# Scores by 64-row products, a later last join of gate and up, and large tiles for every third page step

## Chip, cores, metric

The kernel runs on one core of a Trainium2 chip. The metric is device time of one execution in microseconds: the median of three runs of the kernel before is 2318.37 us (2318.06 to 2319.26).

## What is computed

One inference step of a two-layer decoder, for a prompt of 1024 tokens and for eight samples of one token each (1032 token columns in all, width 1024, everything in float32 precision). Layer 0 mixes by an S5 state-space model beside differential attention, layer 1 by a gated linear recurrence beside causal pooling; each layer ends in a SwiGLU feed-forward network. What the change touches:

```
proj = rmsnorm(x) @ w_in ; u, q, k, v = split(proj) ; q, k = rope(q), rope(k)   # 8 heads of 64
p = softmax(q k^T / 8, causal), per head       # 4 pairs of heads, components c = 0 and 1
o[h] = (p[2h] - lam * p[2h+1]) @ v[h]          # h = 0..3, values 128 wide
# samples: 2048 past keys and values each, in 16 pages of 128 rows, found through page_table
# feed-forward, in both layers:
x = x + (silu(n @ wg) * (n @ wu)) @ wd         # 2816 hidden columns, n = rmsnorm(x)
```

## The kernel before

TensorE works in products of two halves: an operand is split into a rounded part H and a remainder L, and a product is H·H + L·H + H·L (`mm3`, lines 718 to 720). The program is written as one stream of Python calls; a scheduler turns it into a fixed order for each engine, and each engine then runs its list in that order, waiting on semaphores. What decides the time are therefore the order on each engine and the tiles: a tile belongs to a pool with a number of buffers, and whoever fills a tile waits until the last user of the buffer is done.

**The attention stage** (about 325 to 630 us) is the loop at the end of `mixer0`. `order` runs over G = 0, 1 (queries 0 to 511, 512 to 1023) and the four heads h; each (h, G) has four blocks qi of 128 queries. For a block, `attn_scores` makes the two score matrices (c = 0, 1) of 128 queries by nk = (4G+qi+1)·128 keys, takes the maximum on VectorE (DVE) and the exponential on ScalarE (ACT) into tiles P; `attn_values` combines and transposes them (pT to wT, lines 1338 and 1340) and, after the fourth block, multiplies by the values (po, line 1348). Between these calls the loop places three kinds of other work:

- `vsteps`: 32 *page steps* for the samples (`pv`, line 1453). Step c of group g loads four pages of 256 KB from `in_cv`, one for each of four samples, and runs four products of 32 columns, one after the other on four column groups.
- `fill`: the S5 output path (`s5_mix`: tiles z, f, xr, products pd).
- `late`: the first half of the attention's output projection (`attn_mix`: tiles az, ax).

**Page buffers.** The pool `kv` has `KV_BUFS` = 8 buffers of 128x512, so two page steps. Pages are issued on SyncE's queue (SP), in order, by `load_page`.

**Scores before.** Q and K rows of a component are 64 deep. `attn_load` fills a tile Q whose upper 64 rows hold q's H part and whose lower 64 hold its L part, and tiles K (G = 0) or KH, KL (G = 1) in which both halves hold the same 64 rows of k. One product with all 128 rows then gives H·H + L·H, a second one with KL gives the rest; k is fetched twice for this, in pieces of 64 rows. These loads go out on GpSimd's queue (POOL), two `next(nxt)` for each block (`LOADS`), among the loads and stores of `fill` and `late`. The tiles come from the pool `S` (24 buffers of 128x1032), as do P, wT, xr, z and others.

**Feed-forward.** `gate_up` runs 11 pairs j of gate and up products in seven block products each, then `finish(j, ...)`: `normed(u)` (line 404, two multiplications of 128x1032 by the norm), and g·u (line 409, two more). `down` then reads the hidden tiles back (h), builds operands from them (`operands`, lines 475 to 491) and weights (`down_weights`, lines 514, 515), and accumulates products into x (`acc`, line 583).

Of the kernel before, what the change touches and what calls it, by code (L numbers as in the profile page):

```python
# [8 lines left out]
F32 = mybir.dt.float32  # L9
F32R = mybir.dt.float32r  # L10
# [47 lines left out]
NB = 16 // NI  # L58
QUEUES = ("gpsimd", "sync", "sync", "gpsimd", "gpsimd")
Y_BUFS = 11  # L60
LOADS = (2, 2, 2, 2)
MID = 4
KV_BUFS = 8
DENSE = (1, 1, 1, 1, 1, 1, 1, 1)
# [132 lines left out]
class Ffn:  # L197
# [180 lines left out]
    def gate_up(self, S, pp):  # L378
# [69 lines left out]
        for j in range(1, 11):  # L448
            cg, cu = slots(j), slots(j)
            for v, c in ((0, cg), (1, cu)):  # L450
                w = self.load(v, j, S if v else t.wst)
                got = nxt[2 * j - 2 + v] if 2 * j - 2 + v < AHEAD else None
                for p in ORDER:
                    if p != 2 or got is None:
                        self.product(p, w, c, pp, got=got if p == 1 else None)
                if self.l + v == 0 and j == 5:
                    with t.after(self.lastf):
                        t.lru_consts()
                if v == 0:
                    normed(cg)  # L460
                    for x in cg[:2]:
                        nc.scalar.activation(x, x, AF.Silu)
            finish(j, cg, cu)

    def operands(self, h, grp, S):

# [51 lines left out]
    def down(self, xs, S, pp, chunks):  # L518
# [72 lines left out]
        def load_x(n):  # L591
            for m in range(len(xs), n):
                xs.append(t.tile(f"x{m}"))
                nc.sync.dma_start(xs[m], self.xd[m])
# [16 lines left out]
        def prep():  # L611
            ci, grp, p, m = weights.pop(0)
            ms = (m, m + 2) if grp and m % 4 == 0 else (m,)
            for j, mm in enumerate(ms):
                if (ci, grp, mm) not in raws:
                    raws[ci, grp, mm] = raw(ci, mm, grp, j), {}
            if ci + grp == 0 and m == 2 and len(xs) < 8:
                load_x(8)
                for j in range(2):
                    nc.sync.dma_start(self.hd[20 + j], self.last[j])  # L620
            made[ci, grp, p, m] = self.down_weights(p, *raws[ci, grp, m])
# [18 lines left out]
class Trunk:  # L640
# [622 lines left out]
    def attn_load(self, h, G):  # L1263

        nc = self.nc
        n = 512 * G + 512
        self.qk = getattr(self, "qk", {})
        Q = self.tile("Q", F32R)[:, :1024].rearrange("p (c n) -> p c n", c=2)
        ks = []
        self.qk[h, G] = (Q, ks)  # L1270
        for half in range(2):
            src = self.qd[h][half][:, G * 512:G * 512 + 512].bitcast(F32R).rearrange("(c p) n -> p c n", c=2)
            nc.gpsimd.dma_start(Q[half * 64:half * 64 + 64], src)
        yield
        for c in range(2):
            if G:
                ks.append([self.tile(t, F32R)[:, :n] for t in ("KH", "KL")])
            else:
                t = self.tile("K", F32R)
                ks.append([t[:, 0:512], t[:, 512:1024]])  # L1280
            for i in range(2):
                for half in range(2):
                    nc.gpsimd.dma_start(ks[c][i][half * 64:half * 64 + 64],
                                        self.kd[h][i][c * 64:c * 64 + 64, :n].bitcast(F32R))
                yield

    def attn_scores(self, h, G, qi):

        nc = self.nc
        Q, ks = self.qk[h, G]  # L1290
        if qi == 0:
            self.sums = getattr(self, "sums", {})
            self.sums[h, G] = self.sm.tile([128, 2, 4], F32, tag="sums", name="sums")
        sm = self.sums[h, G][:, :, qi]
        nk = (4 * G + qi + 1) * 128
        mx = self.sm.tile([128, 2], F32, tag="mx", name="mx")
        both = None if G else self.sc.tile([128, 2, 512], F32, tag="sc", name="sc")
        P2 = None if G else self.tile("P")
        S, P = [], []
        for c in range(2):  # L1300
            KH, KL = ks[c]
            ql = Q[:, c, qi * 128:qi * 128 + 128]
            ps = self.sc.tile([128, 1024], F32, tag="sc", name="sc") if G else both[:, c]
            for k0 in range(0, nk, 512):
                n = min(512, nk - k0)
                last = k0 + n == nk
                o = ps[:, k0:k0 + n]
                nc.tensor.matmul(o, ql, KH[:, k0:k0 + n], start=True, stop=False)  # L1308
                nc.tensor.matmul(o, ql, KL[:, k0:k0 + n], start=False, stop=not last)
                if last:  # L1310
                    nc.tensor.matmul(o[:, n - 128:n], self.identb, self.maskb, start=False, stop=True)
            if G:
                nc.vector.tensor_reduce(mx[:, c:c + 1], ps[:, :nk], AX.X, ALU.max, negate=True)
            S.append(ps[:, :nk])
            P.append(self.tile(f"P{c}")[:, :nk] if G else P2[:, c * 512:c * 512 + nk])
        if not G:
            nc.vector.tensor_reduce(mx, both[:, :, :nk], AX.X, ALU.max, negate=True)
        for c in range(2):
            nc.scalar.activation(P[c], S[c], AF.Exp, bias=mx[:, c:c + 1], accum_out=sm[:, c:c + 1])
# [63 lines left out]
    def sample_steps(self):  # L1383
# [5 lines left out]
        def page(src, b, c):  # L1389
            t = self.kv.tile([128, 512], F32, tag="kv", bufs=KV_BUFS, name="kv")  # L1390
            self.load_page(t, a[src], b * NPAGE + c)
            return t

        def scores(ch):
            def f():
                if ch == 0:
# [49 lines left out]
        def pv(g, c):  # L1446
            def f():
                if c == 0:
                    st["o"] = self.pst("so", self.pq)
                p = st["o"]  # L1450
                vt = [page("cv", 4 * g + j, c) for j in range(4)]
                w = st["s"][c // 8][:, c % 8 * 128:c % 8 * 128 + 128]
                self.row([lambda j=j: nc.tensor.matmul(  # L1453
                    p[32 * j:32 * j + 32, 0:512], w[:, 32 * j:32 * j + 32], vt[j], start=c == 0, stop=False,
# [595 lines left out]
```

## Time and profile before

| | |
|---|---|
| median of three runs | 2318.37 us |
| the profiled execution's own time | 2323.5 us |
| its span, first to last instruction | 2321.7 us |
| mean granted TensorE clock, as a share of full speed | 0.977 |
| TensorE (PE) busy | 2192.2 us, 94% |
| DVE, ACT, POOL busy | 1605.3, 939.3, 477.4 us |
| chain that ended last | PE 79%, DVE 9%, DMA 7% |

The page's slices and the stage table show where PE is not full. The attention stage, 325 to 630 us, has PE busy for 254.24 of 305 us at a mean granted clock of 0.91. The two places between `gate_up` and `down`, near 1120 and 2070 us, have each one stop of PE of 6.6 us. Nearly everything else runs at a full PE.

### The profile page before, as it was taken

How to read it: one execution, taken by the hardware profiler on the slowest of the kernel's cores; microseconds unless marked ns; L12 is line 12 of the kernel's file. 1: busy time of each engine (PE TensorE's matmuls, PEld its weight loads, DVE VectorE, ACT ScalarE, POOL GpSimd, SP SyncE). 2: the span in 40 equal slices, each digit the busy share in tenths (PEclk: the TensorE clock that was granted, in tenths of full speed). 3: DMA queues.
4: the chain of work that ended last, by engine and by line, in shares of the span. 5: the costliest groups of instructions: out<-in, count | busy, mean ns of one | idle time of the engine just before them, and what ended most of it. 6: DMA issues, size and time to landing. Idle time of an engine off the chain costs nothing.

```text
span 2321.7 us, 44913 instructions
## 1 busy us (share of the span) xinstructions
PE 2192.2 (94%) x17529; PEld 2061.1 (89%) x17529; DVE 1605.3 (69%) x3045; ACT 939.3 (40%) x1746; POOL 477.4 (21%) x585
## 2 busy tenths in 40 slices
PE   6999888887989999999899999999999999989998
PEld 6978766655789999999899998899899999989997
DVE  7879435445687557566999878654956565689966
ACT  5233234333664333333444365543633333344331
POOL 5232322222103333332000000000233333300001
PEclk8999998988999999999999999999999999999999
DMA  6488978998543222222765331334232122266512
GB/s 225 144 262 290 258 227 250 280 272 223 183 152 128 91 74 83 68 82 90 292 218 167 104 84 42 102 114 138 76 107 83 67 82 83 74 239 218 192 64 74
DMA packets 145798, 348.21 MB, mean 150 GB/s; under 512 B 33513, under 2 KB 40554, under 8 KB 145586
## 3 DMA queue, kind: packets, MB, share of 16 engines
q1 hardware_dynamic: 112514, 247.18, 32.4%
q0 software_dynamic: 32496, 97.64, 13.6%
q8 instruction: 138, 2.26, 0.4%
q14 instruction: 74, 0.61, 0.1%
q10 hardware_dynamic: 576, 0.52, 0.1%
HBM read 281.17 MB, written 64.08 MB: 149 GB/s over the span
## 4 chain that ended last, share of the span: by engine, by line
PE 79%; DVE 9%; DMA 7%; ACT 2%; issue 2%; SPq 1%; POOL 1%; DVEq 0%; ACTq 0%; POOLq 0%
PE pd L718 23%; PE pd L720 22%; PE pd L719 22%; DMA kv<-in_cv 3%; DMA kv<-in_ck 2%; PE so L1453 1%; PE po L1348 1%; PE pss L1402 1%; DVE wp L312 1%; DMA xr<-in_x 1%; PE pg L1918 1%; PE pT L1338 1%; PE sc L1308 1%; PE pv L1253 1%; PE pv L1254 1%
## 5 line engine op out<-in xcount | busy, mean ns | idle before, releaser
L720 PE MATMUL pd<-b,wp 128*128 128x256 f32 (+1 forms) x3496 | 987.7, 283 | 14.4 <-DVE wp L515 13.2
L718 PE MATMUL pd<-b,wp 128*128 128x256 f32 (+1 forms) x3496 | 991.7, 284 | 7.6 <-DVE c L373 3.5
L719 PE MATMUL pd<-b,wp 128*128 128x256 f32 (+1 forms) x3496 | 990.7, 283 | 2.3 <-DVE b L275 2.3
L720 PEld LDWEIGHTS pd<-b,wp 128*128 128x128 f32 x3496 | 662.3, 190 | 15.4 <-DVE wp L515 13.6
L718 PEld LDWEIGHTS pd<-b,wp 128*128 128x128 f32 x3496 | 662.6, 190 | 11.0 <-ACT wp L311 3.4
L719 PEld LDWEIGHTS pd<-b,wp 128*128 128x128 f32 x3496 | 662.8, 190 | 3.1 <-DVE b L275 3.1
L331 POOL TENSOR_TENSOR as<-wst 128x512 f32<-128x512 f32 x80 | 136.2, 1702 | 487.5 <-DVE wp L312 328.2
L718 PE MATMUL pd<-xh,wh 128*128 128x344 f32 x576 | 191.1, 333 | 14.7 <-ACT wh L691 10.2
L375 ACT COPY c<-pd 128x512 f32<-128x512 f32 (+1 forms) x260 | 106.1, 444 | 223.0 <-PE pd L720 222.7
L720 PE MATMUL pd<-xh,wl 128*128 128x344 f32 x576 | 188.1, 329 | 4.8 <-DVE wl L692 4.7
L719 PE MATMUL pd<-xl,wh 128*128 128x344 f32 x576 | 188.6, 328 | 0.0
L373 DVE TENSOR_TENSOR c<-pd,c 128x512 f32<-128x512 f32 (+1 forms) x214 | 93.3, 470 | 127.0 <-PE pd L720 126.8
L311 ACT CAST wp<-as 128x512 fp32r<-128x512 f32 x176 | 108.8, 621 | 173.0 <-PE pd L720 164.5
L312 DVE TENSOR_TENSOR wp<-wst,wp 128x512 fp32r<-128x512 f32 x122 | 105.4, 867 | 103.7 <-ACT wp L311 103.7
L312 DVE TENSOR_TENSOR wp<-as,wp 128x512 fp32r<-128x512 f32 x176 | 140.3, 800 | 28.0 <-ACT wp L311 27.9
L404 DVE TENSOR_TENSOR c<-c,R 128x1032 f32<-128x1032 f32 x88 | 110.4, 1255 | 44.9 <-ACT c L375 44.9
L718 PEld LDWEIGHTS pd<-xh,wh 128*128 128x128 f32 x576 | 110.0, 191 | 19.3 <-ACT wh L691 10.6
L583 DVE TENSOR_TENSOR x<-pd,x 128x512 f32<-128x512 f32 x160 | 108.3, 688 | 17.1 <-PE pd L720 15.8
L720 PEld LDWEIGHTS pd<-xh,wl 128*128 128x128 f32 x576 | 109.5, 191 | 8.7 <-DVE wl L692 5.9
L719 PEld LDWEIGHTS pd<-xl,wh 128*128 128x128 f32 x576 | 109.9, 191 | 2.1 <-issue 0.2
L691 ACT CAST wh<-wst 128x1024 fp32r<-128x1024 f32 x58 | 60.7, 1046 | 116.7 <-PE pd L719 85.4
L692 DVE TENSOR_TENSOR wl<-wst,wh 128x1024 fp32r<-128x1024 f32 x58 | 70.8, 1221 | 48.3 <-ACT wh L691 47.9
(537 smaller groups left out, 4075.1 us busy)
## 6 DMA issues: line engine op xcount, KB each, us to landing
h<-hd SPq DMA_DIRECT2D x82, 516.0 KB, 5.8
kv<-in_ck SPq DMA_DIRECT2D x128, 256.0 KB, 4.2
kv<-in_cv SPq DMA_DIRECT2D x128, 256.0 KB, 6.1
wst<-in_w_d SPq DMA_DIRECT2D x48, 512.0 KB, 4.2
wst<-in_w_g SPq DMA_DIRECT2D x46, 512.0 KB, 4.1
wst<-in_w_up SPq DMA_DIRECT2D x44, 512.0 KB, 3.5
hd<-c POOLq DMA_DIRECT2D x40, 516.0 KB, 3.0
wst<-in_w_o POOLq DMA_DIRECT2D x28, 512.0 KB, 4.0
```

The costliest lines, as they stand in the source:

```text
L311: nc.scalar.copy(W[:, 0], s)
L312: nc.vector.tensor_tensor(W[:, 1], s, W[:, 0].bitcast(F32), ALU.subtract)
L331: (nc.vector if self.first else nc.gpsimd).tensor_tensor(s, x, y, op)
L373: V.tensor_tensor(o, i, o, ALU.add)
L375: A.copy(o, i)
L404: nc.vector.tensor_tensor(x, x, t.R, ALU.mult)
L583: nc.vector.tensor_tensor(y, pt[:, :, :256], y, add)
L691: nc.scalar.copy(H, src)
L692: nc.vector.tensor_tensor(L, src, H.bitcast(F32), ALU.subtract)
L718: mm(p, WH, XH, start=first, stop=False, **kw)
L719: mm(p, WH, XL, start=False, stop=False, **kw)
L720: mm(p, WL, XH, start=False, stop=last, **kw)
```

## The change

Four edits:

- **Scores.** Q is now a tile with q's H and L parts side by side, each with both components: component c in rows 64c to 64c+63. K, KH and KL hold the two components the same way, each fetched once. A block's scores are three products of 64 rows for each component and chunk of up to 512 keys (H·H, L·H, H·L), c = 0 and c = 1 taking turns, then the two mask products of 128 rows. The list is issued by `row`, which keeps it together after its first product; both score tiles of a block are taken before it. The maxima follow both.
- **Loads.** `attn_load` has four steps of one DMA each (Q's H, K's H, Q's L, K's L), one for each block (`LOADS`), so that K's L part of a head is issued in the block just before the head's first scores.
- **Page steps.** A step with c % 3 == 2 (10 of 32) loads its four pages into two tiles of the pool `S` and not into `kv`.
- **Last join.** `finish(10)` is called in `down`, when the weights of the second m are prepared, and not at the end of `gate_up`.

```
-LOADS = (2, 2, 2, 2)
+LOADS = (1, 1, 1, 1)
...
-            finish(j, cg, cu)
+            if j < 10:
+                finish(j, cg, cu)
+        self.finish = lambda: finish(10, cg, cu)
...
             if ci + grp == 0 and m == 2 and len(xs) < 8:
+                self.finish()
                 load_x(8)
...
-        for half in range(2):
-            src = self.qd[h][half][:, G * 512:G * 512 + 512].bitcast(F32R).rearrange("(c p) n -> p c n", c=2)
-            nc.gpsimd.dma_start(Q[half * 64:half * 64 + 64], src)
-        yield
-        for c in range(2):
...
-            for i in range(2):
-                for half in range(2):
-                    nc.gpsimd.dma_start(ks[c][i][half * 64:half * 64 + 64],
-                                        self.kd[h][i][c * 64:c * 64 + 64, :n].bitcast(F32R))
-                yield
+        for i in range(2):
+            nc.gpsimd.dma_start(Q[:, i], self.qd[h][i][:, G * 512:G * 512 + 512].bitcast(F32R))
+            yield
+            nc.gpsimd.dma_start(ks[i], self.kd[h][i][:, :n].bitcast(F32R))
+            yield
...
+            for j, (q, k) in enumerate(((0, KH), (1, KH), (0, KL))):
+                for c in range(2):
+                    r = slice(64 * c, 64 * c + 64)
+                    calls.append(lambda c=c, r=r, q=q, k=k, j=j, k0=k0, n=n, last=last: nc.tensor.matmul(
+                        S[c][:, k0:k0 + n], Q[r, q, sl], k[r, k0:k0 + n], start=j == 0, stop=j == 2 and not last))
...
+        self.row(calls)
...
+        def wide(g, c):
+
+            T = [self.tile("kv") for _ in range(2)]
+            vt = [T[j // 2][:, j % 2 * 512:j % 2 * 512 + 512] for j in range(4)]
+            for j in range(4):
+                self.load_page(vt[j], a["cv"], (4 * g + j) * NPAGE + c)
+            return vt
...
-                vt = [page("cv", 4 * g + j, c) for j in range(4)]
+                vt = [page("cv", 4 * g + j, c) for j in range(4)] if c % 3 < 2 else wide(g, c)
```

The lines of the changed kernel stand a few numbers higher than those of before (a page step is line 1463 for 1453). On PE, at the start of the attention stage (so: a page step's four products, sc: scores), before:

```order
L1453 MATMUL so<-kv,ss 32x512 x8
L1308 MATMUL sc<-K,Q 128x128
L1309 MATMUL sc<-K,Q 128x128
L1311 LDWEIGHTS identb
L1311 MATMUL sc<-maskb,identb 128x128
L1308 MATMUL sc<-K,Q 128x128
L1309 MATMUL sc<-K,Q 128x128
L1311 LDWEIGHTS identb
L1311 MATMUL sc<-maskb,identb 128x128
```

and now:

```order
L1463 MATMUL so<-kv,ss 32x512 x12
L1310 MATMUL sc<-K,Q 128x128 x6
L1313 LDWEIGHTS identb
L1313 MATMUL sc<-maskb,identb 128x128
L1313 LDWEIGHTS identb
L1313 MATMUL sc<-maskb,identb 128x128
```

Three page steps stand where two stood, and a block's scores are one run of six products with the two masks behind it.

On POOL's queue, the loads for the last head with G = 1 (kd_111 is k of head 3), before:

```order
L1273 DMA Q<-qd_107 64x2x512 x2
L1283 DMA KH<-kd_111 64x1024 x2
L1089 DMA xp_117<-ax 128x512
L696 DMA wst<-in_w_o 128x1024
L1084 DMA ax<-xp_118 128x512
L1283 DMA KL<-kd_111 64x1024 x2
L1283 DMA KH<-kd_111 64x1024 x2
L1356 DMA ao_113<-od 128x512
L1283 DMA KL<-kd_111 64x1024 x2
```

and now:

```order
L1279 DMA Q<-qd_107 128x512 x2
L1092 DMA xp_117<-ax 128x512
L699 DMA wst<-in_w_o 128x1024
L1087 DMA ax<-xp_118 128x512
L1281 DMA KH<-kd_111 128x1024
L1358 DMA ao_113<-od 128x512
L1092 DMA xp_118<-ax 128x512
L1087 DMA ax<-xp_119 128x512
L1281 DMA KL<-kd_111 128x1024
```

Eight loads of 64 rows have become two of 128, and the last of them stands two entries later than before (behind the store of xp_118 and the load of ax from xp_119).

On DVE, between `gate_up` and `down` of layer 0 (b and h: building `down`'s operands, wp: its weights), before:

```order
L404 TENSOR_TENSOR c<-c,R 128x1032
L484 TENSOR_TENSOR h<-h 128x520
L409 TENSOR_TENSOR c<-c 128x1032
L404 TENSOR_TENSOR c<-c,R 128x1032
L476 TENSOR_TENSOR b<-h,b 128x520
L409 TENSOR_TENSOR c<-c 128x1032
L476 TENSOR_TENSOR b<-h,b 128x512
L476 TENSOR_TENSOR b<-h,b 128x520
L482 TENSOR_TENSOR h<-h 128x512
L515 TENSOR_TENSOR wp<-as,wp 128x512
```

and now:

```order
L486 TENSOR_TENSOR h<-h 128x520
L484 TENSOR_TENSOR h<-h 128x512
L517 TENSOR_TENSOR wp<-as,wp 128x512
L478 TENSOR_TENSOR b<-h,b 128x520
L478 TENSOR_TENSOR b<-h,b 128x512
L478 TENSOR_TENSOR b<-h,b 128x520 x2
L486 TENSOR_TENSOR h<-h 128x520
L517 TENSOR_TENSOR wp<-wst,wp 128x512
L517 TENSOR_TENSOR wp<-as,wp 128x512
L478 TENSOR_TENSOR b<-h,b 128x520
L517 TENSOR_TENSOR wp<-as,wp 128x512
L404 TENSOR_TENSOR c<-c,R 128x1032 x2
```

The four joining multiplications stand behind `down`'s first four weights, no longer ahead of them.

## Rows read from the trace of the kernel before

**Rows 1.** The page, part 1: busy time, share and instructions of each engine.
```profile
PE 2192.2 (94%) x17529; PEld 2061.1 (89%) x17529; DVE 1605.3 (69%) x3045; ACT 939.3 (40%) x1746; POOL 477.4 (21%) x585
```
**Rows 2.** Windows: stretch, busy us by engine, PE clock, DMA share, GB/s.
```profile
325.00:630.00 305.00, 254.24 (x1483) 178.63 (x1483) 156.61 (x358) 123.31 (x305) 74.49 (x134) 0.91 0.85 238
345.00:365.00 20.00, 11.02 (x46) 6.13 (x47) 4.94 (x5) 4.21 (x4) 7.92 (x14) 0.66 1.21 299
```
**Rows 3.** Waits, 325 to 630: who waited for whom, total us, times, longest.
```profile
PE so L1453 <- DMA kv<-in_cv: 40.8, 10, 11.6
POOL xp L1089 <- DVE ax L1087: 31.9, 4, 19.2
PE sc L1308 <- ACT P L1319: 4.1, 5, 1.5
SPq L1380 <- PE so L1453: 57.9, 25, 9.2
```
**Rows 4.** Timeline of PE, page steps: start, length, instruction, idle before.
```profile
339.58 1.08 PE L1453 MATMUL so<-kv,ss 128*32 128x512 f32 x4 [5.64 <-DMA kv<-in_cv]
...
362.65 0.64 PE L1453 MATMUL so<-kv,ss 128*32 128x512 f32 x4 [1.67 <-DMA kv<-in_cv]
...
484.10 1.92 PE L1453 MATMUL so<-kv,ss 128*32 128x512 f32 x16
...
496.44 1.08 PE L1453 MATMUL so<-kv,ss 128*32 128x512 f32 x4 [5.95 <-DMA kv<-in_cv]
...
550.56 1.94 PE L1453 MATMUL so<-kv,ss 128*32 128x512 f32 x8 [11.60 <-DMA kv<-in_cv]
```
**Rows 5.** Timeline of SP's queue, 484 to 490.
```profile
485.17 4.76 SPq L1380 DMA_DIRECT2D kv<-in_cv  x8
```
**Rows 6.** Score products by shape (x count), then two in the timeline.
```profile
L1308 PE MATMUL sc<-KH,Q 128*128 128x512 f32 x40 | 18.8, 469 | 3.5 <-ACT P L1319 3.5
...
503.80 0.40 PE L1308 MATMUL sc<-KH,Q 128*128 128x512 f32 x1
504.04 0.40 PE L1309 MATMUL sc<-KL,Q 128*128 128x512 f32 x1
```
**Rows 7.** Timeline of PE: products of 64 rows in the S5 stage.
```profile
58.95 0.38 PE L1679 MATMUL pK<-CL,s5bb 64*16 64x128 f32 x2
59.16 0.39 PE L1677 MATMUL pK<-CL,s5bb 64*16 64x128 f32 x4
59.38 0.39 PE L1679 MATMUL pK<-CL,s5bb 64*16 64x128 f32 x4
...
114.59 0.50 PE L1785 MATMUL py<-U,TG 128*128 128x136 f32 x2
115.02 0.38 PE L1786 MATMUL py<-H,CL 64*128 64x136 f32 x1
115.03 0.38 PE L1788 MATMUL py<-H,CL 64*128 64x136 f32 x1
```
**Rows 8.** DMA issues, 325 to 630: count, KB each, median us to landing.
```profile
wst<-in_w_o POOLq DMA_DIRECT2D x10, 512.0 KB, 6.6
...
KL<-kd POOLq DMA_DIRECT2D x16, 256.0 KB, 9.9
```
**Rows 9.** Timeline of DVE, then of PE, at the end of layer 0's `gate_up`.
```profile
1120.87 1.23 DVE L409 TENSOR_TENSOR c<-c 128x1032 f32<-128x1032 f32 x1
...
1123.82 0.69 DVE L515 TENSOR_TENSOR wp<-as,wp 128x512 fp32r<-128x512 f32 x1
...
1124.57 0.58 PE L720 MATMUL pd<-b,wp 128*128 128x256 f32 x1 [6.59 <-DVE wp L515]
```
**Rows 10.** `down` of layer 0: windows row as in rows 2; PE's waits 1126 to 1345.
```profile
1120.00:1130.00 10.00, 5.43 (x30) 5.43 (x31) 10.00 (x17) 1.53 (x3) 0.00 (x0) 0.66 0.97 341
1180.00:1200.00 20.00, 20.00 (x171) 20.00 (x170) 19.94 (x36) 9.08 (x16) 0.00 (x0) 1.00 0.79 259
...
PE pd L718 <- DVE x L583: 0.9, 2, 0.5
```

More of the change, by code (lines that the diff above doesn't have):

```diff
@@ L1267, in attn_load @@
         self.qk = getattr(self, "qk", {})
-        Q = self.tile("Q", F32R)[:, :1024].rearrange("p (c n) -> p c n", c=2)
-        ks = []
-        self.qk[h, G] = (Q, ks)
-        for half in range(2):
-            src = self.qd[h][half][:, G * 512:G * 512 + 512].bitcast(F32R).rearrange("(c p) n -> p c n", c=2)
-            nc.gpsimd.dma_start(Q[half * 64:half * 64 + 64], src)
-        yield
-        for c in range(2):
[L1276 to L1280, printed above, removed]
-            for i in range(2):
-                for half in range(2):
-                    nc.gpsimd.dma_start(ks[c][i][half * 64:half * 64 + 64],
-                                        self.kd[h][i][c * 64:c * 64 + 64, :n].bitcast(F32R))
-                yield
+        Q = self.tile("Q", F32R)[:, :1024].rearrange("p (i n) -> p i n", i=2)
+        if G:
+            ks = [self.tile(t, F32R)[:, :n] for t in ("KH", "KL")]
+        else:
+            t = self.tile("K", F32R)
+            ks = [t[:, 0:512], t[:, 512:1024]]
+        self.qk[h, G] = (Q, ks)
+        for i in range(2):
[3 more added lines that the diff above has]
+            yield
     def attn_scores(self, h, G, qi):
         nc = self.nc
-        Q, ks = self.qk[h, G]
+        Q, (KH, KL) = self.qk[h, G]
         if qi == 0:
@@ L1296, in attn_scores @@
         mx = self.sm.tile([128, 2], F32, tag="mx", name="mx")
-        both = None if G else self.sc.tile([128, 2, 512], F32, tag="sc", name="sc")
-        P2 = None if G else self.tile("P")
-        S, P = [], []
-        for c in range(2):
[L1301 to L1315, printed above, removed]
@@ L1316, in attn_scores @@
-        if not G:
+        if G:
+            S = [self.sc.tile([128, 1024], F32, tag="sc", name="sc")[:, :nk] for _ in range(2)]
+            P = [self.tile(f"P{c}")[:, :nk] for c in range(2)]
+        else:
+            both, P2 = self.sc.tile([128, 2, 512], F32, tag="sc", name="sc"), self.tile("P")
+            S = [both[:, c, :nk] for c in range(2)]
+            P = [P2[:, c * 512:c * 512 + nk] for c in range(2)]
+        sl = slice(qi * 128, qi * 128 + 128)
+        calls = []
+        for k0 in range(0, nk, 512):
+            n = min(512, nk - k0)
+            last = k0 + n == nk
+            for j, (q, k) in enumerate(((0, KH), (1, KH), (0, KL))):
[3 more added lines that the diff above has]
+                        S[c][:, k0:k0 + n], Q[r, q, sl], k[r, k0:k0 + n], start=j == 0, stop=j == 2 and not last))
@@ L1317, in attn_scores @@
+        for c in range(2):
+            calls.append(lambda c=c: nc.tensor.matmul(S[c][:, nk - 128:nk], self.identb, self.maskb, start=False, stop=True))
+        self.row(calls)
+        if G:
+            for c in range(2):
+                nc.vector.tensor_reduce(mx[:, c:c + 1], S[c], AX.X, ALU.max, negate=True)
+        else:
             nc.vector.tensor_reduce(mx, both[:, :, :nk], AX.X, ALU.max, negate=True)
```

## Prediction

> **What bounds the kernel now.** I began with the busy shares. TensorE is busy for 94% of the span and DVE for 69% [rows 1], so a change pays where TensorE stands still or runs at the low clock, or where it gives TensorE less to do; what it takes from other engines pays only through those. The windows by stage then say where that is. In the attention stage, 325 to 630 us, TensorE is busy for 254.24 of 305 us at a mean granted clock of 0.91 [rows 2]. So 50.8 us are idle, and, with 1.2 GHz at a half, 18% of the stage (0.09 divided by 0.5), 55 us, lies at the low level. The stretch 345 to 365 is the worst of it: 11.02 of 20 us busy at 0.66.
>
> The waits name the cause. Of the idle time 40.8 us, in ten waits, stand before the page steps (line 1453), each for a page of `in_cv` to land [rows 3]. In the timeline they fall into two kinds. Four lie at the start, from 5.64 us at 339.58 to 1.67 us at 362.65 [rows 4], 15.9 us together: there the pages come in no faster than the steps ask. The other six, 25 us, come after steps that stand close together: two steps run back to back at 484.10, only then are their eight buffers free, SP issues the next eight pages from 485.17 on [rows 5], and TensorE comes to the next step before they are in, 5.95 us of idle time at 496.44; the longest, 11.60 us, is at 550.56 [rows 4]. SP's queue shows the other side of it: 57.9 us in which a page load waited for TensorE to leave a buffer [rows 3]. So the limit is the distance between the issue of a page and its use. Throughput is not full: the stage moves 238 GB/s [rows 2], and `down` has 341 GB/s in one stretch [rows 10].
>
> **The page steps** (part 1). Every third step gets eight pages' worth of room outside the pool of eight: its four pages lie in two tiles of `S`. In the new order three steps stand at the start for two, and where two ordinary steps follow each other, the loads of the next are issued with at least two whole steps between, which by the durations of the work on TensorE's list is 14 to 29 us ahead. The new loads wait for tiles of `S`, whose last users lie 14 us of TensorE work or more ahead of the step. Against a landing of about 12 us (485.17 to the end of the wait at 496.44) that covers the 25 us of the later waits. At the start, the third step is loaded ahead and q and k compete with fewer bytes; there I take off a third, 5 of 15.9. That is **-30 us**, with ends of -12 (half of the later waits goes, the start stays) and -40.8.
>
> The clock follows the waits. At the half level a busy microsecond does half a microsecond's work; 55 us at that level, busy for the same share as 345 to 365 (55%), cost some 15 us (half of 55 x 0.55). If the waits in the middle go, about half of it comes back: **-8**, ends 0 and -15.
>
> **The scores** (part 2). Before there are 32 blocks, each with two components of two products for each chunk: 192 products, 96 of them 512 columns wide and the others 256 on average, 73,700 columns. At full clock two products of 512 start 0.24 us apart [rows 6], so all take 34.6 us. Now there are three for two, 288 products of 64 rows and 110,600 columns: 51.8 us one after another (+17), 25.9 us if the upper and the lower half of the rows work at once (-9). The profile shows which: in the S5 stage two products of 64 rows of one kind take 0.21 us (58.95 to 59.16), and four of one half among four of the other take 0.22 (59.16 to 59.38); and at 115.02 and 115.03 products of two kinds start 0.01 us apart [rows 7]. The halves overlap. What the new form adds is the change between products of 128 and of 64 rows: the two at 114.59 hold TensorE until 115.02, 0.43 us [rows 7], where two without a change on either side take 0.21 to 0.23; 0.2 us for each change. A block changes over twice, into its scores and back for the masks: 64 x 0.2 = 13. Together -9 + 13 = **+4**, with ends of -9 (the overlap alone) and +30 (no overlap, and the changes on top).
>
> Here the Trainium skill speaks against this change: its page "TensorEngine Tiling (Array Packing)" (section "Tiling Modes", Key Properties) says that "Changing tiling mode (not just tile) drains the TensorE", where its "Overview" promises work at once for operands of at most 64 rows. By the promise alone the term would be -9. By a full drain, taken as the length of a product beyond its slot (0.40 less 0.24 in the rows above, an estimate), 64 x 0.16 = 10 would make it +1. The row's 0.2 agrees with a drain and a first weight load that nothing hides.
>
> **The loads of q and k.** 80 loads on POOL become 32, and k comes once. This frees POOL and halves the bytes of k, but POOL and DMA bandwidth are not what TensorE waits for today, so I book no gain but that at the start, above. What it adds is a new race. The last load of a head (KL) is now one DMA of 512 KB for G = 1, issued one block ahead of the first scores that use it, and behind stores that wait for DVE: those of line 1089 hold POOL for 31.9 us in four waits [rows 3]. From the work on TensorE's list between the last thing that its issue waits for and its first use, the four heads of G = 1 leave it 7.4, 11.8, 10.7 and 8.4 us. The nearest rows are 6.6 us for a load of 512 KB and 9.9 us for a KL of 256 KB [rows 8]. At 6.6 nothing is exposed; at twice 9.9, 8 to 12.4 us for each head, some 41 in all. The new load has the bytes and the 128 rows of the first of these, but the company of the second; I take 10 to 11 us, which exposes up to 3 us at a head and about 6 in all, and 4 more for issues that come late: **+10**, ends 0 and +41. Behind a score product that waits stands all of TensorE's list, and after it the exponentials and the transposes of the block.
>
> **Both score tiles at once.** A block's scores now want both buffers before the first product, where the first component could start alone. Today TensorE waits 4.1 us in five waits for the exponential that frees one [rows 3]. I take **+3**, ends 0 and +8 (twice today's wait).
>
> **The last join** (part 3). Between `gate_up` and `down` TensorE stops for 6.59 us, until DVE has made the first weight (line 515, 1123.82 to 1124.51) [rows 9], and the clock over 1120 to 1130 is 0.66 [rows 10], 0.34 x 5.43 = 2 us more. Four multiplications of 1.23 us [rows 9], 4.9 us, stand ahead of that weight on DVE's queue; now they stand behind the first four weights. So the stop shrinks by up to 4.9 us, but the work isn't gone: DVE is busy for 10.00 of 10 us there and for 19.94 of 20 in the middle of `down` [rows 10], where today it holds TensorE for only 0.9 us. What is late next are the accumulations of line 583, with 4.9 us more ahead of them, less the time by which TensorE starts sooner. I take 3 us of gain in each layer: **-6**, ends 0 and -14 (stop and clock of one layer, 7, twice).
>
> **SP's queue.** The loads of a wide step wait for tiles of `S` and hold the ordinary pages behind them. By the order these tiles come free in time: **0**, up to +9 (the longest wait of a page load for a buffer today is 9.2 [rows 3]).
>
> **The sum.** -30 - 8 + 4 + 10 + 3 - 6 = -27. The profiled execution's own time is 2323.5 us, so 2296.5; the median of the runs is 0.9978 of it, which gives 2291 us.
>
> **Rivals.**
> *The page waits stay.* If the transfers themselves are what is slow (the DMA engines have a share of 0.85 in the stage and 1.21 in 345 to 365 [rows 2], so they are seldom idle), a third step in flight only makes each page land later. Then only 12 of the 40.8 go, the clock gives back 2, and KL's wait hides among them: -12 - 2 + 4 + 3 - 6 = -13, so 2305 by the median. Against it: the bytes of k halve, and the later waits begin with an issue that came late.
> *The halves don't overlap.* The change would not do what it says: the scores are +30 and not +4, and the sum is -1, 2317. The rows of the S5 stage speak against it, but those products are short.
> *Slower: KL comes late at every head of G = 1.* It needs twice the 9.9 us of the piece of half its size, and POOL issues it behind a store that DVE holds (up to 19.2 us [rows 3]). With 19.8 us against slacks of 7.4 to 11.8 TensorE stops for 8 to 12.4 us at each head, and a stop of this kind brings the low clock, as the one of 6.59 did for 2 us. With 2 us of late issue at each head that is 41 + 8 + 8 = 57. Without the K term the sum is -37, so +20, 2338. It decides from 37 / 4 = 9 us for a head. For it speaks that the last load of k comes close to its use even today; against it, the row of 6.6 us for 512 KB.
> *Better.* KL lands in time, the changes of mode hide behind the products before them, and all the waits in the middle and half of those at the start go: -33 - 10 - 5 + 1 - 8 = -55, 2263.
>
> **How the numbers follow.** The forecast has a chance of 0.60; pages stay 0.13; no overlap 0.07; KL slower 0.08; better 0.12. The range has to leave out no more than 0.2: the slower rival's upper part and the better one's lower end stay outside, so it goes from 2266 (the page, clock and score terms near their good ends) to 2316 (the no-overlap case just out, KL at half of its bad end in). About 0.2%, 4.6 us, is what a measurement of this kernel can tell from no change, so faster means under 2313.7. Forecast, better and pages-stay lie below it: 0.85. The no-overlap case is the same, 0.07; the rest, 0.08, slower.
>
> **What would show it.** In the changed profile: the waits of page steps (now line 1463) sum to about 11 us, all before 370, against 40.8; the stage's clock is above 0.94 and it ends near 600. In the timeline the products of line 1310 start in pairs, 0.01 us apart, with 0.24 us to the next pair of 512 columns; if 0.24 lies between single ones, the overlap is wrong. Waits of line 1310 for KL are at most 3 us at a head; if 8 and more, the slower rival holds. The stop ahead of `down` shrinks to 2 us, and waits for line 585's sums take up part of it. The forecast is wrong if page steps still wait over 20 us after 370, or if a new wait of the score products for a load or an exponential takes more than 15.

## The result, and the profile after

| | before | changed |
|---|---|---|
| median, each of four runs | 2318.82 us | 2286.25 us (2283.98 to 2289.34) |
| ratio of the runs, 95% interval | 1 | 0.9854 (0.9839 to 0.9868) |
| the profiled execution's own time | 2323.5 us | 2288.0 us |
| TensorE busy | 94% | 96% |

The changed kernel is faster by 1.5%, 5 us below the forecast of 2291 and well inside its range. The reasons given for it hold only in part.

The changed kernel's page, part 1, which answers to [rows 1]:

```profile
PE 2194.5 (96%) x17625; PEld 2059.4 (90%) x17625; DVE 1604.6 (70%) x3045; ACT 939.2 (41%) x1746; POOL 451.0 (20%) x537
```

To compare the attention stage, its ends must be the same pieces of work in both kernels, since everything in it moved. I take it from the first page step to the first product that opens layer 0's feed-forward network: 328.7 to 662.5 us before, 320.9 to 633.0 after. Windows of the kernel before over that stretch (columns as in [rows 2]):

```profile
328.70:662.50 333.80, 279.23 (x1678) 202.99 (x1678) 180.71 (x398) 141.82 (x338) 75.03 (x135) 0.92 0.86 246
```

and of the changed kernel:

```profile
320.90:633.00 312.10, 285.33 (x1773) 204.30 (x1773) 181.31 (x398) 142.48 (x338) 51.45 (x93) 0.93 0.71 242
```

The stage is 21.7 us shorter. Its first step also comes 7.8 us earlier. TensorE's idle time in it fell from 54.6 to 26.8 us (span less busy), and its busy time rose by 6.1. The DMA share fell from 0.86 to 0.71 while the GB/s stayed: the traffic, but for k the same, holds the engines for less time. The column adds up the time of all packets as a share of 16 engines' time; it reaches 1.21 in [rows 2], so 0.86 alone does not say that the engines were full.

TensorE's waits in the changed kernel, 325 to 640 us, which answer to [rows 3]:

```profile
PE so L1463 <- DMA kv<-in_cv: 10.7, 2, 7.6
PE sc L1310 <- ACT P L1321: 4.3, 6, 1.4
PE pd L721 <- ACT ahl L694: 3.8, 2, 2.2
PE pT L1340 <- DVE ax L1090: 3.4, 3, 2.3
```

and the only two page steps that still wait, in its timeline (compare [rows 4]):

```profile
334.33 1.93 PE L1463 MATMUL so<-kv,ss 128*32 128x512 f32 x8 [7.59 <-DMA kv<-in_cv]
...
341.71 1.08 PE L1463 MATMUL so<-kv,ss 128*32 128x512 f32 x4 [3.14 <-DMA kv<-in_cv]
```

Of 40.8 us in ten waits 10.7 in two are left, both at the start. No score product waits for KL.

How far does one execution go? Two kernels below, the join undone and the join spread, differ from the changed kernel only behind this stage, and all engines run the same order in it. Their stages, the join undone first:

```profile
320.30:629.10 308.80, 280.38 (x1773) 200.06 (x1773) 180.73 (x398) 142.69 (x338) 51.43 (x93) 0.96 0.72 245
322.50:627.90 305.40, 277.65 (x1774) 199.03 (x1774) 181.15 (x398) 142.48 (x338) 51.43 (x93) 0.96 0.73 248
```

The idle time repeats (28.4 and 27.8 us beside 26.8). The busy time and the clock do not: 280.4 and 277.7 us at 0.96 beside 285.3 at 0.93. So a difference of a few us in the busy time of one profile is no finding.

The 7.8 us ahead of the stage lie at 282 us, in a part whose TensorE order the change doesn't touch. There the kernel before waits for pages of past keys (waits of TensorE, 235 to 325 us):

```profile
PE pss L1402 <- DMA kv<-in_ck: 6.1, 2, 5.5
```

The changed kernel has no wait in that stretch. What differs there is GpSimd's queue. Before:

```profile
266.57 0.52 POOL L1793 DMA_DIRECT2D zsd<-z  x1
267.08 1.22 POOL L1273 DMA_DIRECT2D Q<-qd  x2
268.26 3.15 POOL L1283 DMA_DIRECT2D K<-kd  x6
```

after:

```profile
267.18 0.52 POOL L1803 DMA_DIRECT2D zsd<-z  x1
283.10 0.56 POOL L699 DMA_DIRECT2D wst<-in_w_o  x1 [15.40 <-DVE wl L695]
```

The ten loads of the first head's q and k stood among the page loads; four loads stand now, from 295 us on, behind two weights and a store of z.

### The profile page after: what moved, and what is told of

Read it like the earlier page. It is cut to its first block, busy times and chain, and to the rows that moved or that the text cites. A ratio compares the mean times of both kernels' runs of the same rounds, so it can differ in the third digit from the quotient of the medians.

```text
span 2286.2 us, 45042 instructions
## 1 busy us (share of the span) xinstructions
PE 2194.5 (96%) x17625; PEld 2059.4 (90%) x17625; DVE 1604.6 (70%) x3045; ACT 939.2 (41%) x1746; POOL 451.0 (20%) x537
## 4 chain that ended last, share of the span: by engine, by line
PE 79%; DVE 10%; issue 4%; DMA 3%; ACT 3%; POOL 1%; SPq 1%; DVEq 0%; ACTq 0%; POOLq 0%
PE pd L721 23%; PE pd L723 23%; PE pd L722 23%; DMA kv<-in_ck 1%; PE po L1350 1%; PE pss L1412 1%; PE so L1463 1%; DVE wp L312 1%; PE sc L1310 1%; DVE b L478 1%; PE pv L1257 1%; PE pv L1255 1%; PE pv L1256 1%; PE pg L1928 1%; DVE b L275 1%
## 5 line engine op out<-in xcount | busy, mean ns | idle before, releaser
L721 PE MATMUL pd<-b,wp 128*128 128x256 f32 (+1 forms) x3496 | 987.6, 283 | 12.2 <-DVE x L585 5.0
L585 DVE TENSOR_TENSOR x<-pd,x 128x512 f32<-128x512 f32 x160 | 108.6, 690 | 13.2 <-PE pd L723 12.2
L311 ACT CAST wp<-wst 128x512 fp32r<-128x512 f32 x122 | 76.4, 629 | 59.2 <-PE pd L723 57.1
```

Source lines behind the costliest of these rows:

```text
L311: nc.scalar.copy(W[:, 0], s)
L585: nc.vector.tensor_tensor(y, pt[:, :, :256], y, add)
L721: mm(p, WH, XH, start=first, stop=False, **kw)
```

## Experiments

All ratios are to the kernel before, measured on the same chip in the same rounds; the changed kernel's own is 0.9854, and 0.001 is 2.3 us. "The stage" has the ends given above.

### Taking the change apart

**The pages alone undone.**

```diff
-                vt = [...] if c % 3 < 2 else wide(g, c)
+                vt = [page("cv", 4 * g + j, c) for j in range(4)]
```

> The changed kernel with all page steps in the pool of eight buffers again; the rest of the change stays. Theory: the later page waits went because the wide tiles let pages be issued earlier. Then the waits of page steps rise from 10.7 us to 35 to 41 us, some of them after 430 us, and the time rises by 25 to 35 us against the changed kernel, to 2311 to 2321. Rival: the waits went because k's bytes are halved and the queues are emptier. Then they stay below 20 us and the time rises by 0 to 8 us.

Measured: 2293.55 us, ratio 0.9872 (0.9856 to 0.9889). Its stage by windows, and its waits:

```profile
321.40:641.60 320.20, 284.83 (x1773) 200.84 (x1773) 182.17 (x398) 143.44 (x338) 51.42 (x93) 0.93 0.71 239
```

```profile
PE so L1463 <- DMA kv<-in_cv: 17.7, 5, 6.0
```

My theory fell, and the rival was right: with the eight buffers of before, page waits are 17.7 us and not 35 to 41. The time is some 4 us above the changed kernel by the ratios (the intervals overlap), the stage 8.1 us longer in the profiles. So scores and loads, without wide pages, shorten the stage by 13.6 us (333.8 to 320.2).

**The scores and loads undone**, pages and join kept: `attn_load`, `attn_scores` and `LOADS` as before.

> The changed kernel with the scores and the loads of q and k of the kernel before (products of 128 rows, k fetched twice, two load steps for each block); wide page steps and late join stay. Theory by the forecast's own terms: the 64-row form costs about 4 us more on TensorE than it saves, and the halved bytes of k are worth nothing; then this kernel is 0 to 8 us faster than the changed one, 2278 to 2286, and TensorE's busy time in the stage falls by about 5 us. Rival: the doubled loads of k put back waits of page steps or of score products, over 10 us of them; then it is 5 to 20 us slower.

Measured: 2307.77 us, ratio 0.9938 (0.992 to 0.9956): 19 us slower than the changed kernel, the rival's side again. Windows and waits of its stage:

```profile
322.20:651.90 329.70, 283.31 (x1677) 206.43 (x1677) 178.74 (x398) 142.08 (x338) 75.09 (x135) 0.92 0.85 249
```

```profile
PE so L1464 <- DMA kv<-in_cv: 12.8, 2, 11.2
PE pT L1341 <- DVE xr L1853: 7.8, 3, 6.8
PE pd L721 <- ACT ahl L694: 5.5, 2, 3.9
```

This is the most telling run. The wide pages do here nearly what I had booked 30 us for: the waits for pages fall from 40.8 to 12.8. Yet the stage is only 4.1 us shorter than before (329.7 against 333.8). TensorE waits for other things instead: in these two rows for xr (a tile whose rows come from memory) and ahl 13.3 us together, and it idles 46.4 us in all, with the DMA share at 0.85 as before.

**The first loads alone moved**, in the kernel before:

```diff
-                    for _ in loads[order[0]]:
-                        pass
+                    with self.after(self.lastz):
+                        for _ in loads[order[0]]:
+                            pass
```

(`lastz` is the last small store of z.) Only GpSimd's order changes, and only in these ten loads.

> The kernel before, with one thing moved: the ten loads of q and k for the first head stand on GpSimd's queue behind the two weight loads and the store of z that followed them, as the loads of the first head do in the changed kernel. No other engine's order changes. Theory: the 7.8 us that the changed kernel gains ahead of the attention stage come from these loads no longer meeting the pages of past keys; then the wait of 5.5 us at 282 us and the low clock after it are gone and the time falls by 6 to 8 us against the kernel before, to about 2311. Rival: that wait was chance of one profiled execution, or the loads then come too late for the first scores: 0, or slower.

Measured: 2314.88 us, ratio 0.9972 (0.9961 to 0.9984), so 6.5 us faster. TensorE's waits, 235 to 325 us, have no page any more:

```profile
PE sc L1309 <- ACT P L1320: 0.6, 1, 0.6
```

This gain is thus the move of the loads, not chance. In the kernel without wide pages the first head's loads stand early again, as four loads of 128 rows, and there the stage also begins 7.3 us earlier than before, with 1.4 us left of the waits for pages of keys: fewer loads cure it nearly as well as later ones.

**The join alone undone**, back to the end of `gate_up`.

> The changed kernel with the last join of gate and up ahead of down again; the rest of the change stays. Theory: the join is worth what the traces of before and after differ by in the two feed-forward networks, 2.3 and 3.4 us, so the time rises by 5 to 6 us, to about 2292, and the stop of 6.6 us ahead of down is back in both layers. Rival: those differences are chance, the join only moves DVE's work: no more than 2 us.

Measured: 2291.14 us, ratio 0.9866 (0.9848 to 0.9884). The intervals overlap, so the times don't settle 5 us. The traces do. From the end of the attention stage to the last instruction this kernel takes 1658.6 us, as the kernel before (1659.2); the changed kernel takes 1653.2, and the other kernels with the late join 1651.0 to 1653.7. And the place is right: the stop of [rows 9] is back (waits of TensorE, 1080 to 1350 us),

```profile
PE pd L720 <- DVE wp L515: 6.6, 1, 6.6
```

where the changed kernel has

```profile
PE pd L721 <- DVE x L585: 2.7, 2, 2.2
PE pd L723 <- DVE wp L517: 1.6, 2, 1.5
```

### What the loads of k cost

After the first two of these runs the question was what in the loads weighs: bytes, form, or the tiles that they hold. Where loads change, the scheduler also places other work a little differently, so differences of a few us may be its doing.

**Form: each load of k cut into two of 64 rows.**

```diff
-            nc.gpsimd.dma_start(ks[i], self.kd[h][i][:, :n].bitcast(F32R))
+            for c in range(2):
+                nc.gpsimd.dma_start(ks[i][64 * c:64 * c + 64], self.kd[h][i][64 * c:64 * c + 64, :n].bitcast(F32R))
```

> The changed kernel with each load of k cut into two of 64 rows: the same bytes, 64 loads on GpSimd's queue instead of 32. New theory after the runs without wide pages and with the old scores: TensorE waited for pages because the DMA engines were held by the pieces of k, and a piece of 64 rows holds them longer for its bytes than a load of 128 rows. Then the DMA share of 325 to 600 us rises from 0.70 by 0.04 or more, pages land later than the median of 4.9 us, and the time rises by 5 to 15 us against the changed kernel (ratio to before 0.987 to 0.992). Rival: only the bytes count, not their form; share and time stay (0.984 to 0.987).

Measured: 2297.05 us, ratio 0.9885 (0.9861 to 0.991), about 7 us slower at equal bytes. The interval touches that of the changed kernel, but each of the four runs (2294.95 to 2299.22) is above each of the changed kernel's, and above each of the run "component after component" below, in the same rounds (2285.53 to 2290.78). The time is that of the theory; one of its signs is not. The DMA share of 325 to 600 us rose from 0.70 to 0.72 only, while pages landed 0.8 us later:

```profile
325.00:600.00 275.00, 248.63 (x1484) 172.63 (x1483) 151.51 (x349) 118.05 (x293) 56.16 (x102) 0.93 0.72 225
```

**Bytes: a second copy that nothing reads.**

```diff
+            nc.gpsimd.dma_start(self.tile('kk', F32R)[:, :n], self.kd[h][i][:, :n].bitcast(F32R))
```

> The changed kernel with a second copy of each load of k into a spare tile that nothing reads: the bytes of k that the kernel before fetched, in loads of 128 rows, 16 more of them on GpSimd's queue. With the run that cuts the loads in two this parts what the old loads cost: form there, bytes here. If the bytes weigh, the DMA share of 325 to 600 us rises from 0.70 by 0.03 to 0.06, pages land about 1 us later, and the time rises by 8 to 15 us (ratio to before 0.989 to 0.992). If it is only the form and the scores' own shape that cost in the old kernel, 0 to 4 us (0.985 to 0.987). A spare tile also takes room in the pool of 24 for a short time, which would add to it.

Measured: 2285.19 us, ratio 0.9839 (0.982 to 0.9858): nothing. Yet the share rose by the 0.06 expected, and pages landed after 6.0 us and not 4.9:

```profile
325.00:600.00 275.00, 249.92 (x1509) 173.03 (x1510) 154.36 (x355) 120.91 (x301) 55.26 (x101) 0.94 0.76 262
```

So neither a share of 0.76 nor pages that land a microsecond later cost time here; and with 262 GB/s the stretch carries more than the 245 of the kernel before, at a lower share.

**Bytes and tiles: a copy for each component, held as long as the first.**

```diff
-        self.qk[h, G] = (Q, ks)
+        self.qk[h, G] = (Q, ks, kc)
...
+            nc.gpsimd.dma_start(kc[i], self.kd[h][i][:, :n].bitcast(F32R))
```

> The changed kernel with k fetched twice in loads of 128 rows, each component's products reading a copy of their own: the bytes of k and the tiles of the pool of 24 that a head of the kernel before takes (five for G = 1), but not its pieces of 64 rows, and the new scores. The run with a spare copy showed that the bytes alone cost nothing. If the held tiles cost (loads and results of the fill work wait for a buffer), the waits of transposes and of the output products rise from 11 to 20 us and more, as with the old scores, and the time rises by 8 to 18 us against the changed kernel (ratio to before 0.989 to 0.993). If not, it stays at 0.983 to 0.987, and what the old scores cost is then the form of their loads and the scores themselves.

Measured: 2288.92 us, ratio 0.9859 (0.9838 to 0.988): nothing either, with pages landing after 6.7 us. So neither k's bytes nor its tiles are what the old loads cost.

The DMA rows of 325 to 600 us show a difference of form. GpSimd's DMA queue (packets, MB, time of its packets as a share of 16 engines) in the kernel before,

```profile
q0 software_dynamic: 12240, 35.22, 46.9%
```

with the old scores and wide pages,

```profile
q0 software_dynamic: 12463, 36.00, 47.2%
```

with k in two held copies,

```profile
q0 software_dynamic: 12624, 37.58, 40.6%
```

with k cut in two,

```profile
q0 software_dynamic: 10610, 31.05, 36.8%
...
kv<-in_cv SPq DMA_DIRECT2D x114, 256.0 KB, 5.7
```

and in the changed kernel:

```profile
q0 software_dynamic: 10589, 31.68, 33.6%
...
kv<-in_cv SPq DMA_DIRECT2D x114, 256.0 KB, 4.9
...
KL<-kd POOLq DMA_DIRECT2D x4, 512.0 KB, 5.2
```

Two fetches of k in pieces of 64 rows hold the DMA engines for 47% of the stretch, two in loads of 128 rows for 41%, though they move more. One fetch in pieces holds them for 36.8%, in whole loads for 33.6%. The Trainium skill has this on its page "SBUF — State Buffer", section "Door 1: The DMA port swizzle": what a DMA can move depends on how many of 16 ports its partitions reach, and 64 neighbouring rows reach half of them. The four shares agree with it.

The pages, whose form never changed, are slowed too. Their queue, in the kernel before and in the changed one without wide pages:

```profile
q1 hardware_dynamic: 17568, 32.01, 41.4%
q1 hardware_dynamic: 17353, 31.46, 34.8%
```

Almost the same bytes hold the engines for 41.4% beside the old loads and for 34.8% beside the new.

How this becomes time is not shown. The run with k cut in two is the slower one at a share of 0.72 and pages landing after 5.7 us, while two copies in whole loads cost nothing at 0.75 to 0.76 and 6.0 to 6.7 us. Its stage is 12.0 us longer than the changed kernel's in the profiles, 6 of it idle time, spread over many waits; and its order on GpSimd and TensorE differs a little. GpSimd's own busy time is not it: 56.2 us of 275 there, 55.3 and 56.9 in the runs with two copies.

**The same rows fetched in one load** (with the old scores): each two pieces become one DMA that reads 64 rows twice.

```diff
-                for half in range(2):
-                    nc.gpsimd.dma_start(ks[c][i][half * 64:half * 64 + 64],
-                                        self.kd[h][i][c * 64:c * 64 + 64, :n].bitcast(F32R))
+                nc.gpsimd.dma_start(ks[c][i], self.kd[h][i][c * 64:c * 64 + 64, :n].bitcast(F32R)
+                                    .unsqueeze(0).broadcast_to([2, 64, n]))
```

> The kernel with the old scores, wide page steps and the late join, but each two pieces of k of 64 rows are one load of 128 rows that reads the same 64 rows twice: the bytes of before, 40 fewer loads. If the form of the pieces is what costs, it gains 8 to 15 us against the one with pieces (ratio to before 0.9938), so 0.987 to 0.990, and the DMA share falls from 0.86 towards 0.75. If the doubled bytes, or the tiles that doubled k holds in the pool of 24, are what costs, it stays within 4 us of it (0.992 to 0.996).

Measured: 2382.55 us, ratio 1.0246 (1.0213 to 1.0279), 71 us slower than with pieces. It doesn't answer its question, since the load is not the one I meant. Its DMA rows, 325 to 600 us, show 24,614 packets under 512 B, where the kernel before has 3,944, and

```profile
KH<-kd POOLq DMA_DIRECT2D x6, 512.0 KB, 25.0
KL<-kd POOLq DMA_DIRECT2D x6, 512.0 KB, 20.7
```

But it acts out the slower rival of the prediction. With loads that land after 20 to 25 us, the score products wait (325 to 740 us):

```profile
PE sc L1311 <- DMA KL<-kd: 27.7, 4, 10.7
PE so L1463 <- DMA kv<-in_cv: 14.4, 3, 6.4
PE pT L1340 <- DVE xr L1852: 14.0, 2, 13.6
```

Four waits for KL, 27.7 us in all, where the rival had four of 8 to 12.4, 41 in all, for a landing of 19.8: its mechanism is real, and what it lacked was a late KL.

### What the 64-row products cost

**Component after component instead of taking turns.**

```diff
-            for j, (q, k) in enumerate(((0, KH), (1, KH), (0, KL))):
-                for c in range(2):
+            for c in range(2):
+                for j, (q, k) in enumerate(((0, KH), (1, KH), (0, KL))):
```

> The changed kernel with the score products of a chunk in the order of the components, three of the upper half of the rows and then three of the lower, instead of taking turns; the other engines' order stays. Theory: products overlap only with a neighbour of the other half; then all but one pair in six run alone, TensorE has 17 to 26 us more work in the stage, and the time rises by 15 to 26 us (ratio 0.992 to 0.997). Rival: TensorE looks further ahead and overlaps them anyway, or the halves don't overlap in the changed kernel either: 0 to 4 us.

Measured: 2286.16 us, ratio 0.9847 (0.9822 to 0.9872), no difference that can be told. One block of it in TensorE's timeline,

```profile
492.93 0.74 PE L1310 MATMUL sc<-KH,Q 64*128 64x512 f32 x4
493.50 0.39 PE L1310 MATMUL sc<-KL,Q 64*128 64x512 f32 x2
493.73 0.40 PE L1310 MATMUL sc<-KH,Q 64*128 64x256 f32 x4
```

and the same block in the changed kernel:

```profile
489.87 0.73 PE L1310 MATMUL sc<-KH,Q 64*128 64x512 f32 x4
490.44 0.39 PE L1310 MATMUL sc<-KL,Q 64*128 64x512 f32 x2
490.67 0.40 PE L1310 MATMUL sc<-KH,Q 64*128 64x256 f32 x4
```

Both are alike: the first six products of 512 columns take 0.80 us (489.87 to 490.67, and 492.93 to 493.73), where six of 0.24 us one after another would take 1.44. In the kernel of this run the program's order is twice KH, KH, KL, yet all four KH start ahead of both KL. The halves do overlap, whatever the order.

**The masks amid the products**, so that each block changes between 64 and 128 rows four times, not twice.

```diff
+                if last and j == 1:
+                    for c in range(2):
+                        calls.append(... nc.tensor.matmul(S[c][:, nk - 128:nk], self.identb, self.maskb, start=False, stop=False))
```

(and none behind them)

> The changed kernel with the two mask products of 128 rows of each block in the midst of the 64-row products of its last chunk instead of behind them: TensorE changes between products of 64 and of 128 rows four times for a block instead of twice, 64 more changes. Theory: a change costs 0.2 us, so 13 us more work, and the time rises by 9 to 14 us (ratio 0.989 to 0.992). Rival: the cost lies elsewhere or is hidden, 0 to 3 us.

Measured: 2296.53 us, ratio 0.9878 (0.9852 to 0.9905), beside 0.9847 for the one above in the same rounds: about 7 us, and busy time 12 us above that of the changed kernel (windows of the stage):

```profile
321.50:644.90 323.40, 297.56 (x1773) 205.33 (x1773) 181.23 (x398) 142.44 (x338) 51.42 (x93) 0.93 0.70 233
```

Each of its four runs (2291.11 to 2298.95) is above each of that one's. For 64 more changes that is 0.11 us each by the time and 0.19 by the busy time, both at a clock of 0.93; the 0.2 of the forecast was at the upper end. The Trainium skill's rule of a drain at each change (the page cited in the prediction) agrees in that the changes have a price; that it is a drain, no run here shows.

### Two tries at more

**The fourth page step wide too**: `c % 3 < 2 and (g, c) != (0, 3)`.

> The changed kernel with one more wide page step, the fourth of all, so that four steps stand ready at the start. If the two waits left (7.6 us at 334 us, 3.1 us at 342 us) come from pages issued only when the first step had left its buffers, the first of them goes and the time falls by 4 to 9 us (ratio to before 0.9815 to 0.984). If the DMA engines are what is short at the start, the wait moves to the next steps or to other work and the time stays within 3 us.

Measured: 2293.32 us, ratio 0.9868 (0.9847 to 0.9889): no gain. Two waits of page steps are left, 8.7 us, the longest still at the fourth step:

```profile
332.76 1.94 PE L1463 MATMUL so<-kv,ss 128*32 128x512 f32 x8 [7.72 <-DMA kv<-in_cv]
...
325.28 18.73 SPq L1382 DMA_DIRECT2D kv<-in_cv  x15
```

The second row says why this run does not answer its question. A wide step needs no page buffer, but the last two of the fourth step's pages were issued from 325.28 us on, the very last at 326.4, where the changed kernel issues it at 326.1. SyncE issues these pages 1.2 us apart, as it looks up each one's row in `page_table` first; from 485.17 us on, in [rows 5], it was 0.6. Whether earlier pages would end the wait stays open.

**The join's four multiplications spread**: one ahead of each of four weights (`next(self.finish, None)` in `prep`).

> The changed kernel with the four multiplications of the late join spread, one ahead of each of four weights of down's second m, instead of all four behind one another. TensorE now waits 2.2 us for the accumulations behind them and 1.5 us for a weight, in each layer. If those waits come from the four in a row, they shrink to below 1.5 us together and the time falls by 2 to 5 us over both layers (0.983 to 0.9845). If DVE is simply full there, they move to other weights or sums and the time stays within 2 us.

Measured: 2282.27 us, ratio 0.9826 (0.9803 to 0.9848): no difference from the changed kernel that its interval clears. Its waits at layer 0's `down` (1080 to 1350 us) are others, not fewer:

```profile
PE pd L731 <- ACT wp L527: 1.9, 1, 1.9
PE pd L733 <- DVE wp L528: 1.6, 2, 1.5
```

## Why the prediction held, and where it didn't

Each term of the sum beside what the two profiles differ by. The stage is 21.7 us shorter: 27.8 of idle time less, 6.1 of busy time more. By the runs' medians the gain is 32.6 us, of which the profiles' 35.5 is one draw.

| term | forecast | measured |
|---|---|---|
| page waits | -30 | -30.1 (40.8 to 10.7) |
| KL's wait, both score tiles, SP | +13 | +2.3 (the rest of the idle time) |
| clock and scores, in the busy time | -4 | +6.1 |
| last join, both layers | -6 | -6.0 (all behind the stage, 1659.2 to 1653.2) |
| ahead of the stage | 0 | -7.8 |
| sum | -27 | -35.5 |

**Page waits.** The size was right and the cause half right. I said that the limit is the distance between a page's issue and its use. For the page waits that holds: the run with old scores has the new distance and none of the middle waits, though its pages land after 8.1 us (6.4 before). But it gains only 4 us in the stage, since other waits take the place of these. And the run without wide pages has the old distance, and its waits are 17.7. The wide steps add to the new loads some 8 us in the profiles (4 by the ratios).

The step that failed stands in two places: "Throughput is not full", and with it "POOL and DMA bandwidth are not what TensorE waits for today", by which the new loads were booked at no gain but 5 us at the start. They alone shorten the stage by 13.6 us, and without them the change is 19 us slower. It is not the GB/s that were full: the run with a second copy carries 262 at no cost. What is shown to count is the form in which the bytes travel. The rival "the page waits stay" named the DMA share; its time was wrong, since it gave the change no relief of it.

Of the 19 us, 7 are shown to be the form: one fetch in pieces costs that, while bytes and tiles cost nothing. The score products take TensorE the same time in both forms, 54.4 and 54.6 us (below). That the second copy in pieces makes up the rest, and the order of the old scores nothing, was not parted and stays open; so does by which wait the pieces cost their time.

**KL.** I took 10 to 11 us to land, nearest to the pieces; it took 5.2. The form is not the whole reason: cut into pieces of 64 rows in the changed kernel, KL still landed after 5.5 us and KH after 8.8 (6.2 whole). A landing time read beside the old loads did not carry over to a kernel without them. The waits for KL that I put at 10 us were none in the changed kernel, and one of 1.4 in the execution with the join undone.

**Clock and scores.** The clock's term was too large, and that of the scores can't be told to a few us. The score products and masks take TensorE 54.38 us before and 54.55 now (windows of the stage for the tile sc):

```profile
328.70:662.50 333.80, 54.38 (x256) 0.92 0.86 246
320.90:633.00 312.10, 54.55 (x352) 0.93 0.71 242
```

That is +0.2 and not +4. But a part of the price of a change falls on the neighbours: with the masks amid the products these rows rise by 8.6 us, to 63.12, and the busy time by 12.2. So +4 is not excluded. For the clock I took -8. In the profile of the changed kernel the mean clock went from 0.92 to 0.93 only and the busy time rose by 6.1; in the two executions of the same order shown above it is 0.96, and the busy time differs from before by +1.2 and -1.6. With scores of +0.2 to +4, the clock gave back at most 6 us in these two and nothing in the first; what it gives in the median run can't be told from so few profiles. TensorE also falls to half where it hardly waits (windows of the changed kernel):

```profile
484.00:494.20 10.20, 9.41 (x65) 7.71 (x64) 4.54 (x11) 3.04 (x7) 0.53 (x1) 1.00 0.79 282
494.20:501.00 6.80, 6.80 (x28) 5.63 (x27) 4.64 (x13) 3.49 (x11) 0.00 (x0) 0.50 0.00 0
```

6.80 of 6.80 us busy at half speed, behind a stretch that was busy for 9.41 of 10.20. In both executions of the same order the clock over 485 to 505 us is 1.00: the same order ran there without the fall.

**Join.** Right in size and mechanism. Before, the stop of 6.59 us and 0.9 of other waits stood there in layer 0 [rows 9, 10]; now 4.3 stand there, for sums and weights, with DVE as full as it was (10.00 of 10 us from 1090 on).

**Ahead of the stage.** Missed. The order on GpSimd's queue showed the first head's loads moved behind two weights and a store; I costed loads only where TensorE used them, not among the page loads they left.

So the total came out in part by luck. 18 us of gain were missing (KL and the other waits 10.7, the place ahead 7.8), and against them stands what clock and scores gave less than booked: 10 us in these two profiles, 2 to 5 by the other two executions.

## What to carry to other kernels

Look at the form of the loads before the GB/s: 238 GB/s were no sign of room here, since with k in whole loads the same engines moved more (262) at a lower share (0.76 for 0.89). But the share is no price either: 0.72 with pieces was slower than 0.76 without. A wait that is prefetched away can come back elsewhere, as with the old loads it did at xr and ahl. Where a change moves a load, cost the place that it leaves too. And before a term of a few us is read from the busy time or the clock, look at a second execution of the same order.

## What I had not expected of the hardware

Products of the two halves of the rows overlap whatever their order in the program: with three products of one half ahead of three of the other in the program, the other half's first two still started ahead of the first half's third, and six took 0.80 us both ways. Doubling k's bytes in loads of 128 rows cost nothing (0.9839), cutting the single copy into loads of 64 rows about 7 us, and a DMA that reads 64 rows twice made six times the small packets and landed after 21 to 25 us.
